# Sixteen pairs by seven products in both FFNs, the last chunk's weight sums made inside the FFN

## The chip, the cores and the metric

The kernel runs on one core of one Trainium2 chip. The metric is the device time of one execution in microseconds (us), lower is better. Before the change it is 1126.34 us, the median of 3 runs (1126.19 to 1126.67).

The engines are TensorE (PE, matmuls; its weight loads are shown as PEld), VectorE (DVE), ScalarE (ACT), GpSimd (POOL) and SyncE (SP, which only issues transfers). Each has its own queue of instructions and works through it in order; they wait for each other by semaphores.

## What is computed

A causal decoder of two layers on 512 tokens of width 1024, all in float32. Layer 0 has latent and differential attention, layer 1 dilated and stick-breaking attention; after each comes a gated FFN with a causal convolution of width 3. The change touches only the FFNs:

```python
def causal_dwconv(h, w, b):          # width 3, each channel by itself
    y = lax.conv_general_dilated(h, w[:, None, :].astype(h.dtype), (1,), [(CONV_WIDTH - 1, 0)],
                                 dimension_numbers=('NWC', 'WIO', 'NWC'), feature_group_count=c)
    return y + b

def conv_ffn(h, w_up, conv_w, conv_b, w_down):
    u = causal_dwconv(h @ w_up, conv_w, conv_b)
    gate, up = jnp.split(u, 2, axis=-1)
    return (jax.nn.silu(gate) * up) @ w_down
```

`h` is 512 x 1024, `w_up` 1024 x 5632 (2816 gates and 2816 ups), `w_down` 2816 x 1024.

## The kernel before, in words

**Float32 from parts.** Each operand is split into a high part (a cast to fp32r on ACT) and a low part (the difference, on DVE); a product is three matmuls, high by high, high by low and low by high (`mm3`, lines 315 to 317). A *unit* of weights is 128 x 1024 numbers. The class `Weights` loads it into one of three raw buffers (`wraw`, issued by SP, lines 57 and 59), then splits it (line 81 on ACT, line 82 on DVE) into one of five pairs of buffers, `wh` and `wl`. `W.depth` says how many units are prepared ahead in the order of the code.

**The FFN.** The 22 gate channels' blocks of 128 and the 22 of the ups are worked through as 22 *pairs* n = 0 to 21, a gate block and an up block each. Two pairs together form one k = n // 2 of the down product.

- Pairs 0 and 1 use the first four units.
- A *plain* pair multiplies each of its two blocks (z = 0, 1) with the whole of `x`: 8 blocks of the depth, 3 matmuls of 512 columns each; two units.
- A *seven-product* pair (function `seven`) takes gate and up as one 2 x 2 block product by the scheme of seven products in place of eight (Strassen's, in Winograd's form). Each product has 4 blocks of the depth and 3 matmuls of 256 columns. The sums of `x` blocks are made once in the FFN (`x_sums`, tiles `sums`). Sums and differences of weight blocks are not made on the engines but in memory, by accumulating transfers on POOL's queue (`sum_steps`, line 161): four arrays of sums from four arrays of blocks, `ws`, held in *chunks* of three pairs. Each chunk takes 8 transfers; step by step they depend on each other. A pair reads 7 blocks of 256 KB (line 57), so 3.5 units.

`SEVEN` says which pairs are by seven products: 4 to 17 in FFN 0 and 4 to 15 in FFN 1. The sums for FFN 0 are made while layer 0's attention runs (three calls, chunks 0 to 4), those for FFN 1 while layer 1's attention runs (line 1498). A one-element transfer from a value that is computed at the right moment (the `mark`) goes ahead and holds the first transfer back until then.

After each pair come its scaling (line 492, ACT), convolution (496 and 498, DVE), silu (502, ACT) and the products of gate and up; after every second pair the steps `second` to `fifth` form the blocks of the down product's left side. `fifth` splits one result into a tile of `g_tile` (11 of them; four hold `sums` until the last seven-product pair) and appends it to `early`. In the seven-product stage the order of PE, DVE and ACT is written by hand (`manual_schedule`); steps that find no tile free are put in `late` and run behind the stage. In the other stages a planner sets the order, from its own costs.

**The down product.** It runs over k = 0 to 10 in two parts. In the first, each step k uses `early[k]` and two units made by `down_weights` (line 351 and 354, sums of weight blocks on DVE; then the split), 24 matmuls of 512 columns into banks `acc`. For k below 3 there is one more copy and add (702 and 703). In the second part the results `later` are used; `split_later` (line 223 and 224, `gh` and `gl` from `hold`) prepares them.

**What the code's lines show.** Line 559 is a copy on ACT that stands once in every seven-product pair, line 577 another; 585 and 596 are DVE's additions of products.

## Time and profile before

| | |
|---|---|
| median of 3 runs | 1126.34 us |
| the profiled execution's own time | 1127.14 us |
| its span (first to last instruction) | 1125.4 us |
| PE busy | 1114.6 us, 99% |
| PEld busy | 955.6 us, 85% |
| DVE busy | 889.2 us, 79% |
| ACT busy | 631.0 us, 56% |
| POOL busy | 109.4 us, 10% |

In FFN 0 the seven-product pairs start at 282.88 us of the span and the down product at 467.71; in FFN 1 at 826.95 and 1013.39.

How to read the rows: a row of the timeline has start, duration, engine, line, operation, what it writes and reads with shapes, and in brackets the idle time of the engine before it and what ended it. A row of the table by stretches has for each engine the busy time and, in brackets, how many instructions; then the granted clock of PE (1.00 is full), the share of the DMA engines' time and the rate. A row of the transfers has what is written and read, the issuing queue, how many, their size and the median time from issue to landing. Matmuls overlap in PE, so their durations are longer than the distance between their starts. Line numbers are those of the kernel before.

### The profile page before, as it was taken

The page shows a single profiled execution, that of the slowest core. Times are in us where ns is not written, and L with a number is a line of the kernel's source. Part 1 is how long each engine was busy: PE and PEld are TensorE (multiplying, and loading weights), DVE is VectorE, ACT ScalarE, POOL GpSimd, SP SyncE. Part 2 cuts the span into 40 slices and gives each one's busy share as a digit, 9 for nine tenths or more (in the row PEclk, how much of TensorE's full clock was granted, in tenths as well). Part 3 has the DMA queues.
Part 4 walks back from the last instruction along what each step waited for, and adds up shares of the span by engine and source line. Part 5 has one row for each costly group of instructions (what it writes and reads, how often), then busy time and mean ns, then how long its engine had stood idle before and what let it go on. Part 6 is the DMA issues. An engine that isn't in the chain of part 4 may idle for free.

```text
span 1125.4 us, 17611 instructions
## 1 busy us (share of the span) xinstructions
PE 1114.6 (99%) x6576; PEld 955.6 (85%) x6576; DVE 889.2 (79%) x1504; ACT 631.0 (56%) x1070; POOL 109.4 (10%) x214
## 2 busy tenths in 40 slices
PE   9999999999999999999999999999999999999997
PEld 8866777898999998888888877888999999888886
DVE  6677466489899999899974476677889999789896
ACT  5565466446566665456544454565466666445662
POOL 2311133220000000000031112002000000000002
PEclk9999999999999999999999999999999999999999
DMA  8797898542556554355738999922336555334461
GB/s 296 236 256 186 246 269 204 158 135 94 161 177 187 178 185 141 108 153 164 243 98 267 300 287 291 250 77 98 94 104 196 176 182 190 111 100 144 139 206 75
DMA packets 66406, 201.48 MB, mean 179 GB/s; under 512 B 9105, under 2 KB 10257, under 8 KB 59665
## 3 DMA queue, kind: packets, MB, share of 16 engines
q1 hardware_dynamic: 56928, 143.34, 39.0%
q0 software_dynamic: 7904, 54.53, 19.0%
q10 hardware_dynamic: 1488, 2.49, 0.7%
q8 instruction: 52, 0.85, 0.3%
q14 instruction: 34, 0.27, 0.1%
HBM read 192.95 MB, written 60.85 MB: 226 GB/s over the span
## 4 chain that ended last, share of the span: by engine, by line
PE 88%; DVE 5%; DMA 2%; issue 2%; ACT 2%; POOL 0%; SPq 0%; POOLq 0%; DVEq 0%; ACTq 0%
PE u L315 12%; PE u L316 12%; PE u L317 12%; PE acc L315 4%; PE acc L316 4%; PE acc L317 4%; PE apt L315 3%; PE apt L316 3%; PE apt L317 3%; PE ao L315 2%; PE ao L317 2%; PE ao L316 2%; DVE wl L82 2%; PE sps L1115 2%; PE av L317 1%
## 5 line engine op out<-in xcount | busy, mean ns | idle before, releaser
L81 ACT CAST wh<-wraw 128x1024 fp32r<-128x1024 f32 x237 | 245.3, 1048 | 155.6 <-PE u L316 51.1
L82 DVE TENSOR_TENSOR wl<-wraw,wh 128x1024 fp32r<-128x1024 f32 x237 | 287.3, 1219 | 56.9 <-ACT wh L81 55.5
L315 PE MATMUL u<-xh,wh 128*128 128x256 f32 (+1 forms) x664 | 212.1, 319 | 0.0
L316 PE MATMUL u<-xl,wh 128*128 128x256 f32 (+1 forms) x664 | 211.8, 319 | 0.0
L317 PE MATMUL u<-xh,wl 128*128 128x256 f32 (+1 forms) x664 | 211.7, 319 | 0.0
L315 PEld LDWEIGHTS u<-xh,wh 128*128 128x128 f32 x664 | 126.5, 191 | 9.0 <-ACT wh L81 0.3
L317 PEld LDWEIGHTS u<-xh,wl 128*128 128x128 f32 x664 | 126.5, 190 | 8.9 <-DVE wl L82 0.3
L316 PEld LDWEIGHTS u<-xl,wh 128*128 128x128 f32 x664 | 126.5, 191 | 8.6
L316 PE MATMUL acc<-wl,gh 128*128 128x512 f32 (+1 forms) x250 | 96.9, 387 | 0.0
L317 PE MATMUL acc<-wh,gl 128*128 128x512 f32 (+1 forms) x250 | 96.8, 387 | 0.0
L315 PE MATMUL acc<-wh,gh 128*128 128x512 f32 (+1 forms) x250 | 96.8, 388 | 0.0
L315 PE MATMUL u<-gh,wh 128*128 128x256 f32 x312 | 88.3, 283 | 0.0
L317 PE MATMUL u<-gh,wl 128*128 128x256 f32 x312 | 88.3, 283 | 0.0
L316 PE MATMUL u<-gl,wh 128*128 128x256 f32 x312 | 88.3, 283 | 0.0
L230 POOL TENSOR_TENSOR rv<-ms,epst 128x1 f32<-128x1 f32 x39 | 12.1, 309 | 758.6 <-ACT junk L282 372.1
L492 ACT ACTIVATE y<-u,cw 128x512 f32<-128x512 f32 x88 | 67.5, 776 | 14.7 <-PE u L317 14.7
L496 DVE SCALAR_TENSOR_TENSOR y<-u,cw,y 128x511 f32<-128x511 f32 x88 | 65.0, 742 | 5.2 <-ACT y L492 5.2
L498 DVE SCALAR_TENSOR_TENSOR y<-u,cw,y 128x510 f32<-128x510 f32 x88 | 65.5, 746 | 2.3
L315 PEld LDWEIGHTS u<-gh,wh 128*128 128x128 f32 x312 | 59.9, 192 | 0.2
L316 PEld LDWEIGHTS u<-gl,wh 128*128 128x128 f32 x312 | 59.9, 192 | 0.1
L317 PEld LDWEIGHTS u<-gh,wl 128*128 128x128 f32 x312 | 59.9, 192 | 0.0
L315 PEld LDWEIGHTS acc<-wh,gh 128*128 128x128 f32 x250 | 46.9, 188 | 10.1 <-issue 0.6
(364 smaller groups left out, 2432.7 us busy)
## 6 DMA issues: line engine op xcount, KB each, us to landing
ws<-in_ffn_up_q POOLq DMA_DIRECT2D x48, 768.0 KB, 12.8
wraw<-ws SPq DMA_DIRECT2D x104, 256.0 KB, 3.0
wraw<-in_ffn_w_down SPq DMA_DIRECT2D x44, 512.0 KB, 3.6
wraw<-in_ffn_up_q SPq DMA_DIRECT2D x78, 256.0 KB, 2.9
wraw<-in_ffn_w_up SPq DMA_DIRECT2D x36, 512.0 KB, 3.7
ws<-ws POOLq DMA_DIRECT2D x16, 768.0 KB, 13.6
wraw<-in_od_w_dqk SPq DMA_DIRECT2D x12, 512.0 KB, 11.4
wraw<-in_ffn_w_down SPq DMA_DIRECT2D x22, 256.0 KB, 2.9
```

Of the source, the lines that this page charges most:

```text
L81: self.nc.scalar.copy(h[:, :w], raw[:, :w])
L82: self.nc.vector.tensor_tensor(l[:, :w], raw[:, :w], h[:, :w].bitcast(F32), ALU.subtract)
L230: POOL.tensor_tensor(v[:, :n], ms, epst[:, :n], ALU.add)
L315: PE.matmul(o, lh, rh, start=first, stop=False, skip_group_check=more)
L316: PE.matmul(o, lh, rl, start=False, stop=False, skip_group_check=more)
L317: PE.matmul(o, ll, rh, start=False, stop=last, skip_group_check=more)
L492: ACT.activation(y[:, z], u[z], AF.Identity, bias=c[:, 3:4], scale=c[:, 2:3])
L496: DVE.scalar_tensor_tensor(y[:, z, 1:], u[z][:, :S - 1], c[:, 1:2], y[:, z, 1:], ALU.mult, ALU.add)
L498: DVE.scalar_tensor_tensor(y[:, z, 2:], u[z][:, :S - 2], c[:, 0:1], y[:, z, 2:], ALU.mult, ALU.add)
L1115: PE.matmul(s_ps[:, :w], mq[h][:, i * P:(i + 1) * P], mk[h][:, :w], start=True, stop=True)
```

## The change

`SEVEN` becomes pairs 4 to 19 in both FFNs, so two plain pairs are left behind them in each. The sizes of the chunks are listed: FFN 0 has (3, 3, 3, 3, 2, 2), FFN 1 (3, 3, 3, 3, 4). The last chunk of each, `OWN`, is made inside the FFN itself, from the moment at which the gate of pair 0 has been scaled; the other chunks are made where they were. `fifth` of k = 7 takes a pair of weight buffers in place of a `g_tile`, one more step runs at once where it was put in `late`, and the lookahead behind the seven-product pairs is one less.

```diff
-SEVEN = range(4, 18), range(4, 16)
-CHUNK = 3
+SEVEN = range(4, 20), range(4, 20)
 PAIRS = [len(n) for n in SEVEN]
-CHUNKS = [-(-n // CHUNK) for n in PAIRS]
+CHUNKS = (3, 3, 3, 3, 2, 2), (3, 3, 3, 3, 4)
+PLACE = [[(c, i) for c, n in enumerate(sizes) for i in range(n)] for sizes in CHUNKS]
+OWN = (5,), (4,)
...
                 else:
-                    src = A[f"ffn_up_q{layer}"][src, c * CHUNK * P:c * CHUNK * P + n]
-                nc.gpsimd.dma_start(tiles[j][c][:n].rearrange(wide, q=4), src.rearrange(wide, q=4), accum_op=op,
+                    at = sum(CHUNKS[layer][:c]) * P
+                    src = A[f"ffn_up_q{layer}"][src, at:at + CHUNKS[layer][c] * P]
+                nc.gpsimd.dma_start(tiles[j][c][:].rearrange(wide, q=4), src.rearrange(wide, q=4), accum_op=op,
                                     max_dma_last_dim=8192)
...
-                return sums_of[layer][j - 4][i // CHUNK][i % CHUNK * P:(i % CHUNK + 1) * P]
+                c, i = PLACE[layer][i]
+                return sums_of[layer][j - 4][c][i * P:(i + 1) * P]
...
                     def fifth():
-                        g = g_tile()
+                        g = W.pair() if len(early) == HF - 4 else g_tile()
...
-                    if heavy and n < 2 * (HF - 4) + 2:
+                    if heavy and n < 2 * (HF - 3) + 2:
                         rest[3]()
                     elif heavy:
                         late.append(rest[3])
...
                             written.__exit__(None, None, None)
-                            W.depth = depth
+                            W.depth = depth - 1
...
                         if z == 0 or n != pairs[0] - 1:
                             scale(z)
+                        if n == z == 0 and OWN[layer]:
+                            ACT.copy(lead[0:1, 2 + layer:3 + layer], y[0:1, 0, 0:1])
+                            make_sums(layer, OWN[layer], lead[0:1, 2 + layer:3 + layer])
...
-                make_sums(1, range(CHUNKS[1]), lead[0:1, 1:2])
+                make_sums(1, range(4), lead[0:1, 1:2])
```

More of the change, by code (lines that the diff above doesn't have):

```diff
@@ L148, in sum_steps @@
             if layer not in sums_of:
-                sums_of[layer] = [[dpool.tile([CHUNK * P, S], F32, tag=f"ws{layer}{j}{c}", name="ws")
-                                   for c in range(CHUNKS[layer])] for j in range(4)]
+                sums_of[layer] = [[dpool.tile([n * P, S], F32, tag=f"ws{layer}{j}{c}", name="ws")
+                                   for c, n in enumerate(CHUNKS[layer])] for j in range(4)]
             tiles = sums_of[layer]
             def move(c, j, src, op):
-                n = min(CHUNK, PAIRS[layer] - c * CHUNK) * P
                 if src is None:
-                    src = tiles[0][c][:n]
+                    src = tiles[0][c][:]
                 elif src < 0:
-                    src = tiles[1][c][:n]
+                    src = tiles[1][c][:]
                 else:
-                    src = A[f"ffn_up_q{layer}"][src, c * CHUNK * P:c * CHUNK * P + n]
-                nc.gpsimd.dma_start(tiles[j][c][:n].rearrange(wide, q=4), src.rearrange(wide, q=4), accum_op=op,
+                    at = sum(CHUNKS[layer][:c]) * P
+                    src = A[f"ffn_up_q{layer}"][src, at:at + CHUNKS[layer][c] * P]
+                nc.gpsimd.dma_start(tiles[j][c][:].rearrange(wide, q=4), src.rearrange(wide, q=4), accum_op=op,
                                     max_dma_last_dim=8192)
```

## The prediction, made before the result was known

> **What bounds the kernel now.** I read the page's busy times first, then the busy time of each engine by stretches of one FFN, then the timelines of ScalarE (ACT), VectorE (DVE) and TensorE (PE) around the stage that changes, and last the table of transfers.
>
> ```profile
> PE 1114.6 (99%) x6576; PEld 955.6 (85%) x6576; DVE 889.2 (79%) x1504; ACT 631.0 (56%) x1070; POOL 109.4 (10%) x214
> ```
>
> ```profile
> core 0: us, PE busy (x) PEld busy (x) DVE busy (x) ACT busy (x) POOL busy (x), PEclk, DMA share, GB/s
> ...
> 321.00:341.00 20.00, 20.00 (x169) 20.00 (x168) 18.77 (x27) 13.18 (x18) 0.00 (x0) 1.00 0.60 184
> ...
> 436.00:447.00 11.00, 11.00 (x50) 9.13 (x49) 8.96 (x12) 5.53 (x8) 0.00 (x0) 1.00 0.23 73
> ...
> 475.00:486.00 11.00, 11.00 (x51) 9.09 (x50) 11.00 (x14) 6.64 (x8) 0.00 (x0) 1.00 0.48 139
> 486.00:497.00 11.00, 11.00 (x50) 9.13 (x49) 11.00 (x15) 6.46 (x8) 0.00 (x0) 1.00 0.58 183
> 497.00:508.00 11.00, 11.00 (x51) 9.09 (x50) 8.69 (x12) 5.30 (x7) 0.00 (x0) 1.00 0.51 142
> 508.00:519.00 11.00, 11.00 (x50) 9.13 (x49) 10.27 (x15) 7.31 (x11) 0.00 (x0) 1.00 0.30 93
> 519.00:530.00 11.00, 11.00 (x50) 8.98 (x49) 9.93 (x14) 7.14 (x10) 0.00 (x0) 1.00 0.73 243
> ```
>
> The stretches are FFN 0: 321 to 341 lies in the pairs by seven products, 436 to 447 in the plain pairs, 475 to 530 in the first part of the down product. PE is busy without a break at a granted clock of 1.00 in all of them, so PE's own work is the path. DVE is the one engine near it: 94% in the seven-product pairs, all of the time from 475 to 497.
>
> How long a pair takes is read from ACT, which does one thing at a fixed place of each pair.
>
> ```profile
> 310.43 0.36 ACT L559 COPY u<-u 128x256 f32<-128x256 f32 x1 [2.01 <-PE u L317]
> ...
> 411.21 0.36 ACT L559 COPY u<-u 128x256 f32<-128x256 f32 x1 [1.90 <-PE u L317]
> ...
> 440.49 1.05 ACT L81 CAST wh<-wraw 128x1024 fp32r<-128x1024 f32 x1 [2.39 <-PE u L316]
> ...
> 462.25 1.05 ACT L81 CAST wh<-wraw 128x1024 fp32r<-128x1024 f32 x1 [3.19 <-PE u L316]
> ```
>
> L559 runs once per seven-product pair; from 310.43 to 411.21 are ten pairs, so one takes 10.08 us. The two casts each wait for PE to free a weight buffer, four plain weight units apart: 21.76 / 4 = 5.44 us a unit, 10.88 a plain pair.
>
> **The change part by part.** *Six pairs change form (two in FFN 0, four in FFN 1).* A plain pair is 2 halves x 8 blocks x 3 = 48 matmuls of 512 columns, one each 227 ns; the other form is 7 x 4 x 3 = 84 of 256, one each 120 ns. A pair saves 10.88 - 10.08 = 0.80 us of PE, six save 4.8 us, all of it on the path as long as PE stays fed. The Trainium skill (TensorE: Matmul & The Clock Gate, Back-to-back issue gap) gives N/2.4 + 2.5 ns for an isolated gap: by that 10.36 and 9.17 us a pair, 7.1 us for six. The rows of this case are 13 ns a matmul above it in both forms, and I take the rows.
>
> *DVE and ACT in those pairs.* A seven-product pair has 3.5 weight units to split where a plain one has 2. DVE stays at 94% there, so a longer stretch of the same kind costs nothing. PE stands in front of it: if that cover went, each of the 1.5 extra splits would cost 1.2 us.
>
> *What comes after the seven-product pairs.* Now FFN 0 has four plain pairs there and FFN 1 six; afterwards both have two. They are where DVE gets ahead of PE. Also, one of the five weight buffers is taken from pair 16 on by a split result (the eighth of `early`, until step 7 of the down product), so four are left, and the lookahead is cut from 5 to 4. The down product's tightest place today:
>
> ```profile
> 467.71 0.39 PE L315 MATMUL acc<-wh,gh 128*128 128x512 f32 x1
> ...
> 467.70 1.05 ACT L81 CAST wh<-wraw 128x1024 fp32r<-128x1024 f32 x1 [0.97 <-PE u L316]
> ...
> 468.78 1.23 DVE L82 TENSOR_TENSOR wl<-wraw,wh 128x1024 fp32r<-128x1024 f32 x1 [0.85 <-ACT wh L81]
> 469.92 0.74 DVE L496 SCALAR_TENSOR_TENSOR y<-u,cw,y 128x511 f32<-128x511 f32 x1
> ...
> 473.62 0.42 DVE L525 TENSOR_TENSOR y<-y 128x256 f32<-128x256 f32 x1
> 473.96 0.41 DVE L528 TENSOR_TENSOR y<-y 128x256 f32<-128x256 f32 x1
> ...
> 479.98 1.22 DVE L82 TENSOR_TENSOR wl<-wraw,wh 128x1024 fp32r<-128x1024 f32 x1
> 481.12 0.68 DVE L351 TENSOR_TENSOR wraw<-wraw 128x512 f32<-128x512 f32 x1
> 481.72 1.22 DVE L82 TENSOR_TENSOR wl<-wraw,wh 128x1024 fp32r<-128x1024 f32 x1
> ```
>
> Call 467.71, the first matmul of the down product, s. A step k of it takes 24 matmuls, 5.44 us, and uses its second unit first (wl in its second matmul, 0.23 later). Step 3 needs it at s + 16.32 + 0.23 = 484.26; its split (481.72) ends at 482.94, 1.3 us early. In FFN 1 it is the same place:
>
> ```profile
> 1013.39 0.39 PE L315 MATMUL acc<-wh,gh 128*128 128x512 f32 x1
> ...
> 1027.39 1.22 DVE L82 TENSOR_TENSOR wl<-wraw,wh 128x1024 fp32r<-128x1024 f32 x1
> ```
>
> There 1028.61 against 1029.94, also 1.3, though six plain pairs lie ahead: the buffers, not the plain pairs, set it. With four buffers the second unit of step 1 gets the buffer that the last plain unit frees, so its cast starts at s (today that cast belongs to step 2) and DVE takes it 1.08 later. In the changed program's order of instructions DVE has between it and step 3's second split, that one included: 5 pieces of 1024 columns, 2 of the convolution, 10 of 512 and 4 of 256. From start to start these take 1.14, 0.70, 0.60 and 0.34 (481.12 less 479.98, 0.04 under the duration 0.74, 481.72 less 481.12, 473.96 less 473.62): 5.70 + 1.40 + 6.00 + 1.36 = 14.5. The step 1 split starts at s + 1.08 and holds DVE for 1.14, the 14.5 follow, the last split among them with its full 1.22: its end is at s + 1.08 + 1.14 + 14.5 + 0.08 = s + 16.8, 0.2 late; today's stretch from 468.78 to 482.94 runs 0.3 over the same kind of sum, so 0.5 late. Bounds: nothing (DVE loses none of its 1.3 us) to 2.3 (below). I take 0.5 for each FFN, 1.0. Behind it come, for steps 4 to 8, 10 pieces of 1024, 2 of 768 (under 1.14 each), 17 of 512 and 3 of 256: 11.4 + 2.3 + 10.2 + 1.0 = 24.9 us against PE's 5 x 5.44 = 27.2, so DVE recovers. FFN 1 also gets one split (1.14) put behind its last seven-product pair, as FFN 0 has it today; it lies under the plain pairs.
>
> *The last chunk's sums, made in the plain pairs.* Eight transfers in memory for each FFN, 512 KB in FFN 0 and 1 MB in FFN 1, a one-element transfer ahead of them, and one ACT copy of one element (under L559's 0.36 us, beside PE). POOL has nothing else to do until the end of the FFN (POOL is at 0.00 in every stretch above), so nothing queues behind their waits there. The other chunks keep their sizes and places.
>
> ```profile
> 260.21 2.78 ACT L492 ACTIVATE y<-u,cw 128x512 f32<-128x512 f32 x4 [0.87 <-PE u L317]
> 282.88 0.28 PE L315 MATMUL u<-xh,wh 128*128 128x256 f32 x1
> ...
> 804.29 2.79 ACT L492 ACTIVATE y<-u,cw 128x512 f32<-128x512 f32 x4 [0.88 <-PE u L317]
> 826.95 0.28 PE L315 MATMUL u<-xh,wh 128*128 128x256 f32 x1
> ```
>
> ```profile
> q0 software_dynamic: 7904, 54.53, 19.0%
> ...
> ws<-in_ffn_up_q POOLq DMA_DIRECT2D x48, 768.0 KB, 12.8
> wraw<-ws SPq DMA_DIRECT2D x104, 256.0 KB, 3.0
> wraw<-in_ffn_w_down SPq DMA_DIRECT2D x44, 512.0 KB, 3.6
> ...
> wraw<-in_od_w_dqk SPq DMA_DIRECT2D x12, 512.0 KB, 11.4
> ...
> ws<-ws POOLq DMA_DIRECT2D x2, 512.0 KB, 4.8
> ```
>
> They start when the first pair is scaled (261 and 805) and form a chain of six dependent steps, 4.8 to 12.8 us each by these rows: done by 265 + 77 = 342 in FFN 0 and 886 in FFN 1 at the latest, needed at 282.88 + 14 x 10.08 = 424 and 826.95 + 12 x 10.08 = 948. In time. But they run on into the seven-product pairs, whose loads (60% of the DMA time) they share. 19.0% of 1125 us for 54.5 MB is 3.9 us of all engines per MB: 33 us in FFN 1, 16 in FFN 0, of which the lightly loaded plain pairs can take half or more. PE is 3.9 us behind the splits (first plain unit: split ends 420.13, used at 424.0) and that absorbs a short delay:
>
> ```profile
> 418.90 1.23 DVE L82 TENSOR_TENSOR wl<-wraw,wh 128x1024 fp32r<-128x1024 f32 x1 [1.32 <-ACT wh L81]
> ```
>
> Bounds 0 to 6.3 us (below); I take 0.4, near the lower end, because only one or two transfers are in flight where the 11.4 us row had a crowd.
>
> *Moved loads.* On SP, each changed pair issues seven loads of 256 KB in place of two of 512 KB; loads on SP wait for raw buffers as now. Cost nothing, under PE.
>
> Sum: 4.8 - 1.0 - 0.4 = 3.4 us. The profiled execution took 1127.14 with a span of 1125.4, 0.8 above the median; span 1122.0, median 1126.34 - 3.4 = **1122.9**. What a measurement can tell is about 0.2%, 2.25 us.
>
> **The rivals.** *All of it arrives:* DVE reaches step 3 in time, the transfers are hidden. For it: 1.3 us in hand at step 3 today. Against: four buffers. 1126.34 - 4.8 = 1121.5.
>
> *DVE becomes the bound of the down product.* DVE is full from 475 to 497, and idle 11 + 11 + 11 - 8.69 - 10.27 - 9.93 = 4.1 us from 497 to 530, waiting for loads and casts. If these waits stay, with four buffers, steps 4 to 8 need 24.9 + 4.1 = 29.0 against 27.2: 1.8 more, 2.3 for each FFN. 4.8 - 4.6 - 0.4 = -0.2: 1126.5, no change.
>
> *Slower: the transfers starve the seven-product pairs.* Three raw buffers turn over once per load, cast and split; 8.64 us are there for three units (3 x 2.88), cast and split take 2.3, so it decides when loads take over 6.3 us on average. They take 3.0 now (3.6 for 512 KB), and 11.4 for 512 KB in the stretch where the other sums are made. At 11.4 each round of three loses 11.4 + 2.3 - 8.64 = 5.1 us; two rounds in FFN 1, less the 3.9 of the lead, give 6.3: 1122.5 + 6.3 = 1128.8. The Trainium skill (DMA: Bandwidth & Descriptors, Queues, rings and completion order) says that each DMA engine goes round between the queues that have work, a packet at a time; by that a load does not wait for a whole transfer, but shares with it, which the rise from 3.6 to 11.4 agrees with. Against it: at most two of the new transfers at a time.
>
> *The sums come late,* so pairs 16 to 19 wait and the time grows by what is missing: they have 62 us in hand at least by the bounds above. Some 1128 and up.
>
> **How the numbers follow.** All of it 0.20; forecast 0.42 (1121.9 to 1124.2 by itself); DVE bound 0.18; starved loads 0.13; late or something not seen 0.07. Faster by 0.2% (under 1124.1): the first and nearly all of the second, 0.60. Within: the rest of the second and most of the third, 0.20. Slower: 0.20. The range 1121.3 to 1128 leaves out the dearer part of the last two.
>
> **What would show it.** In the profile after: L315 to L317 together 216 more; L559's copy (some lines lower) every 10.08 us, 32 times; first `acc` matmul of FFN 0 near 465.9; no DVE wait on `in_ffn_w_down` beyond 1 us; a PE gap of about 0.5 us some 16 us behind each first `acc`. Wrong: PE gaps in the first seven-product pairs of FFN 1 with ACT waiting on `wraw` loads above 6 us (starved), gaps at every step of the down product (DVE bound), or another time per pair than 10.08.

## The result, and the profile after

| | median us | lowest to highest | runs |
|---|---|---|---|
| before | 1126.12 | 1125.62 to 1126.67 | 6 |
| after | 1130.86 | 1128.11 to 1132.55 | 6 |

After against before is 1.0043, 95% interval 1.0032 to 1.0053: slower by 4.7 us, where 1122.9 was forecast. The profiled execution after took 1130.34 us, with a span of 1128.2. The two profiled executions, which the stages below are read from, differ by 2.8 us of span: that of before lies 0.8 above its median, that of after 0.5 below its own.

First the page of the kernel after, busy times, software queue and a load's landing (issues, KB each, median us). PE has 6792 - 6576 = 216 matmuls more, as the step on the pairs had it. The software queue moved 67.12 MB where it moved 54.53.

```profile
PE 1112.5 (99%) x6792; PEld 963.3 (85%) x6792; DVE 901.7 (80%) x1525; ACT 643.6 (57%) x1093; POOL 119.1 (11%) x232
...
q0 software_dynamic: 9760, 67.12, 23.6%
...
wraw<-ws SPq DMA_DIRECT2D x128, 256.0 KB, 3.0
```

The timeline of PE after, at the edges of the stages: the first seven-product matmul of FFN 0, its first and its last `acc`, and the same of FFN 1 (the lines stand two lower than before, so L317 to L319 are the old L315 to L317).

```profile
281.94 0.28 PE L317 MATMUL u<-xh,wh 128*128 128x256 f32 x1
...
465.17 0.39 PE L317 MATMUL acc<-wh,gh 128*128 128x512 f32 x1
...
572.20 0.39 PE L319 MATMUL acc<-gh,gl 128*128 128x512 f32 x1
...
825.48 0.28 PE L317 MATMUL u<-xh,wh 128*128 128x256 f32 x1
...
1014.83 0.39 PE L317 MATMUL acc<-wh,gh 128*128 128x512 f32 x1
...
1120.77 0.28 PE L319 MATMUL acc<-wh,gl 128*128 128x256 f32 x1
```

Of before the same places are in the prediction, but for the last `acc` of each FFN:

```profile
573.67 0.39 PE L317 MATMUL acc<-gh,gl 128*128 128x512 f32 x1
...
1118.19 0.28 PE L316 MATMUL acc<-wl,gh 128*128 128x256 f32 x1
```

The last one read off for the last `acc` of FFN 1 is 1118.31, one matmul (0.12) behind this row. So the time went:

| stage | before | after | difference |
|---|---|---|---|
| FFN 0, first seven-product matmul to first `acc` | 184.83 | 183.23 | -1.60 |
| FFN 0, first to last `acc` | 105.96 | 107.03 | +1.07 |
| FFN 0's last `acc` to FFN 1's first seven-product matmul | 253.28 | 253.28 | 0 |
| FFN 1, first seven-product matmul to first `acc` | 186.44 | 189.35 | +2.91, where -3.20 was due |
| FFN 1, first to last `acc` | 104.92 | 105.94 | +1.02 |

The rest is -0.94 ahead of FFN 0's stage, where the code is the same but for the small copy and the start of FFN 0's own transfers, and +0.37 behind the last `acc`.

Where FFN 1's stage loses 6.1 us is seen in the copy that ACT makes once in each seven-product pair (L561, formerly L559). The timeline of ACT after:

```profile
832.92 0.37 ACT L561 COPY u<-u 128x256 f32<-128x256 f32 x1
845.11 0.37 ACT L561 COPY u<-u 128x256 f32<-128x256 f32 x1
857.55 0.36 ACT L561 COPY u<-u 128x256 f32<-128x256 f32 x1 [1.90 <-PE u L319]
868.01 0.36 ACT L561 COPY u<-u 128x256 f32<-128x256 f32 x1
879.28 0.36 ACT L561 COPY u<-u 128x256 f32<-128x256 f32 x1 [2.48 <-PE u L319]
889.36 0.36 ACT L561 COPY u<-u 128x256 f32<-128x256 f32 x1 [1.16 <-PE u L319]
```

The steps are 12.19, 12.44, 10.46, 11.27 and 10.08. Against 10.08 that is 2.11 + 2.36 + 0.38 + 1.19 = 6.04 us, and after 879 nothing more. Stretches of the kernel after over the first two of these pairs (columns: us; PE, PEld, DVE, ACT, POOL busy; granted clock; DMA share; GB/s):

```profile
825.50:836.00 10.50, 10.50 (x89) 10.50 (x88) 6.67 (x13) 4.56 (x8) 0.82 (x1) 1.00 0.91 298
836.00:842.60 6.60, 6.60 (x57) 6.60 (x56) 4.88 (x6) 4.00 (x6) 0.00 (x0) 1.00 1.03 236
842.60:846.00 3.40, 0.41 (x4) 0.23 (x2) 1.81 (x3) 2.82 (x4) 0.54 (x1) 0.91 1.09 355
846.00:849.00 3.00, 3.00 (x15) 3.00 (x16) 2.44 (x4) 0.58 (x1) 0.00 (x0) 0.53 0.88 319
```

And of before at the same place:

```profile
826.90:835.00 8.10, 8.10 (x69) 8.06 (x69) 4.76 (x7) 3.50 (x7) 0.00 (x0) 1.00 0.21 75
835.00:842.60 7.60, 7.60 (x66) 7.60 (x65) 6.97 (x12) 6.29 (x9) 0.00 (x0) 1.00 0.48 140
```

The DMA engines are full where they were at a quarter to a half. PE stops for 3 us; the 3 us behind that touch 15 matmuls, where 27 would fit (one each 0.12 us, and two over the edges), at a granted clock of 0.53. Who keeps PE waiting is told by the chain of work between 825 and 870 after (start, us, what):

```profile
815.90 16.04 DMA wraw<-in_ffn_up_q
831.97 1.06 ACT wh L82
833.05 1.23 DVE wl L83
...
834.67 8.36 DMA wraw<-ws
843.11 1.05 ACT wh L82
844.19 1.23 DVE wl L83
845.42 0.35 DVE u L587
...
851.39 9.19 DMA wraw<-in_ffn_up_q
```

Three loads of 256 KB on the path took 16.04, 8.36 and 9.19 us; the page's median is 3.0. What PE itself waits for is not the split but L587 (formerly L585), the addition of products that stands behind the split in DVE's order and whose bank PE goes on with (timeline of PE after):

```profile
845.90 0.56 PE L317 MATMUL u<-gh,wh 128*128 128x256 f32 x1 [2.99 <-DVE u L587]
```

Beside the loads the transfers for the last chunk's sums run, issued by POOL (timeline of POOL after, each with the wait for the one before it):

```profile
834.22 0.82 POOL L162 DMA_DIRECT2D ws<-in_ffn_up_q  x1 [9.04 <-DMA ws<-ws]
...
851.27 0.82 POOL L162 DMA_DIRECT2D ws<-in_ffn_up_q  x1 [7.46 <-DMA ws<-ws]
```

The chain's first transfer starts at 807.74 and its last at 851.27; the other long gap, 1.32 us at 867, has the load of 9.19 us in its chain, issued beside the last transfer.

### The profile page after: what moved, and what is told of

Same layout as the page of the kernel before. It is cut to its first block, busy times and chain, and to the rows that moved or that the text cites. A ratio compares the mean times of both kernels' runs of the same rounds, so it can differ in the third digit from the quotient of the medians.

```text
span 1128.2 us, 18178 instructions
## 1 busy us (share of the span) xinstructions
PE 1112.5 (99%) x6792; PEld 963.3 (85%) x6792; DVE 901.7 (80%) x1525; ACT 643.6 (57%) x1093; POOL 119.1 (11%) x232
## 3 DMA queue, kind: packets, MB, share of 16 engines
q0 software_dynamic: 9760, 67.12, 23.6%
## 4 chain that ended last, share of the span: by engine, by line
PE 80%; DVE 9%; DMA 5%; issue 3%; ACT 2%; POOL 0%; SPq 0%; POOLq 0%; DVEq 0%; ACTq 0%
PE u L317 11%; PE u L319 11%; PE u L318 11%; DVE wl L83 4%; PE apt L317 3%; PE apt L318 3%; PE acc L317 3%; PE apt L319 3%; PE acc L318 2%; PE acc L319 2%; DMA wraw<-in_ffn_up_q 2%; PE ao L317 2%; PE ao L319 2%; PE ao L318 2%; DMA wraw<-in_ffn_w_down 2%
## 5 line engine op out<-in xcount | busy, mean ns | idle before, releaser
L83 DVE TENSOR_TENSOR wl<-wraw,wh 128x1024 fp32r<-128x1024 f32 x246 | 298.6, 1220 | 44.9 <-ACT wh L82 43.4
L82 ACT CAST wh<-wraw 128x1024 fp32r<-128x1024 f32 x246 | 254.8, 1047 | 128.1 <-PE u L318 24.2
L317 PE MATMUL u<-xh,wh 128*128 128x256 f32 (+1 forms) x640 | 195.3, 305 | 0.0
L319 PE MATMUL u<-xh,wl 128*128 128x256 f32 (+1 forms) x640 | 195.3, 305 | 0.0
L318 PE MATMUL u<-xl,wh 128*128 128x256 f32 (+1 forms) x640 | 195.1, 305 | 0.0
L319 PEld LDWEIGHTS u<-xh,wl 128*128 128x128 f32 x640 | 122.5, 191 | 5.5 <-DVE wl L83 0.7
L317 PEld LDWEIGHTS u<-xh,wh 128*128 128x128 f32 x640 | 122.6, 192 | 4.9
L317 PE MATMUL u<-gh,wh 128*128 128x256 f32 x384 | 109.6, 285 | 4.3 <-DVE u L587 4.3
L318 PE MATMUL u<-gl,wh 128*128 128x256 f32 x384 | 109.4, 285 | 0.0
L319 PE MATMUL u<-gh,wl 128*128 128x256 f32 x384 | 109.3, 285 | 0.0
L317 PE MATMUL acc<-wh,gh 128*128 128x512 f32 (+1 forms) x234 | 90.6, 389 | 0.5 <-DVE uu L704 0.5
L319 PE MATMUL acc<-wh,gl 128*128 128x512 f32 (+1 forms) x234 | 90.8, 388 | 0.0
L317 PEld LDWEIGHTS u<-gh,wh 128*128 128x128 f32 x384 | 74.3, 193 | 4.8 <-ACT u L561 4.7
L318 PEld LDWEIGHTS u<-gl,wh 128*128 128x128 f32 x384 | 74.3, 194 | 0.1
L319 PEld LDWEIGHTS u<-gh,wl 128*128 128x128 f32 x384 | 74.3, 194 | 0.0
L162 POOL DMA_DIRECT2D ws<-in_ffn_up_q x66 | 47.8, 726 | 155.6 <-DMA ws<-ws 75.1
```

What stands on the lines that cost most here:

```text
L82: self.nc.scalar.copy(h[:, :w], raw[:, :w])
L83: self.nc.vector.tensor_tensor(l[:, :w], raw[:, :w], h[:, :w].bitcast(F32), ALU.subtract)
L162: nc.gpsimd.dma_start(tiles[j][c][:].rearrange(wide, q=4), src.rearrange(wide, q=4), accum_op=op, max_dma_last_dim=8192)
L317: PE.matmul(o, lh, rh, start=first, stop=False, skip_group_check=more)
L318: PE.matmul(o, lh, rl, start=False, stop=False, skip_group_check=more)
L319: PE.matmul(o, ll, rh, start=False, stop=last, skip_group_check=more)
```

## The experiments

Each kernel here was run beside the kernel before. This table holds the stages as they are read above, from the profiled execution of each, and the times; the sections below take them one by one. "Due" is before less 0.80 us for each changed pair.

| run | FFN 0 sevens | FFN 0 `acc` | FFN 1 sevens | FFN 1 `acc` | median us | ratio to before (95%) |
|---|---|---|---|---|---|---|
| before | 184.84 | 105.96 | 186.44 | 104.92 | | |
| due with 16 and 16 pairs | 183.24 | | 183.24 | | | |
| after | 183.23 | 107.03 | 189.35 | 105.94 | 1130.86 | 1.0043 (1.0032 to 1.0053) |
| sums in the attention | 183.22 | 106.70 | 183.26 | 106.53 | 1149.71 | 1.0208 (1.0194 to 1.0222) |
| no transfers | 183.25 | 106.96 | 183.24 | 105.79 | 1123.78 | 0.9981 (0.9972 to 0.9991) |
| FFN 0 only | 183.36 | 106.71 | 186.46 | 104.92 | 1125.51 | 0.9998 (0.9989 to 1.0007) |
| two small chunks | 183.24 | 106.86 | 193.04 | 106.30 | 1129.83 | 1.0033 (1.0023 to 1.0044) |
| buffers only | 184.91 | 106.03 | 186.46 | 105.75 | 1127.81 | 1.0016 (1.0008 to 1.0025) |
| moved to idle | 183.22 | 106.24 | 183.24 | 106.21 | 1130.68 | 1.0038 (1.0026 to 1.0050) |
| fourteen pairs | 183.24 | 107.50 | 184.98 | 105.06 | 1126.43 | 1.0005 (0.9996 to 1.0013) |
| FFN 0 with 1 MB | 190.97 | 106.81 | 187.71 | 106.44 | 1135.86 | 1.0089 (1.0067 to 1.0110) |
| between the norms | 183.65 | 106.89 | 183.22 | 106.48 | 1125.22 | 0.9994 (0.9985 to 1.0003) |
| spaced | 183.32 | 106.95 | 189.88 | 106.30 | 1132.18 | 1.0054 (1.0041 to 1.0066) |
| one split later | 183.38 | 105.91 | 183.22 | 105.26 | 1122.83 | 0.9974 (0.9965 to 0.9983) |
| two splits later | 183.26 | 106.16 | 183.22 | 105.86 | 1124.18 | 0.9983 (0.9974 to 0.9992) |

### No transfers: are they the cause?

```diff
-OWN = (5,), (4,)
+OWN = (5,), ()
...
-                c, i = PLACE[layer][i]
+                c, i = PLACE[layer][i - 12 if layer and i > 11 else i]
```

> The changed kernel without the last chunk's transfers in FFN 1: pairs 16 to 19 of FFN 1 load the sums of pairs 4 to 7, so the same loads are issued and the eight transfers are left out (the sums of four pairs are those of others). Theory 'starved loads': FFN 1's seven-product stage takes 183 to 184 us, attention is as before, time 1126.1 - 4.8 + 2 = 1123.3. Rival 'four buffers': stage 188 us or more, time near 1130. The difference to the kernel with the transfers in attention is what they cost there.

This kernel leaves out the sums of pairs 16 to 19, so it does not compute the function; it stands here for its time alone.

1123.78. FFN 1's stage takes 183.24 us, to the hundredth what was due. Against after, 1130.86 - 1123.78 = 7.1 us by the medians (6.9 when each is taken against the before of its own set of runs): that is the price of eight transfers of 1 MB. In the profiled executions 6.1 of it is in the stage. The stretch that was full in the kernel after, in this kernel:

```profile
825.50:836.00 10.50, 10.50 (x89) 10.46 (x88) 7.12 (x13) 4.88 (x8) 0.00 (x0) 1.00 0.30 90
836.00:842.60 6.60, 6.60 (x58) 6.60 (x57) 6.00 (x8) 5.57 (x8) 0.00 (x0) 1.00 0.48 160
```

The DMA share is at 0.30 and 0.48 instead of 0.91 and 1.03, with the same weight loads. The four weight buffers are those of the kernel after, so they are not what FFN 1's stage lost by.

How little a late load needs to stop PE is seen in the same pair of this kernel, on DVE and on PE:

```profile
842.19 0.42 DVE L587 TENSOR_TENSOR u<-u,y 128x256 f32<-128x256 f32 x1
```

```profile
842.93 0.28 PE L317 MATMUL u<-gh,wh 128*128 128x256 f32 x1
```

The addition ends at 842.61, 0.3 us before PE goes on with its bank. It comes right behind a split (L83). By these rows a load that lets this split start more than 0.3 us late stops PE, however far the splits themselves are ahead of PE.

### FFN 0 only

```diff
-SEVEN = range(4, 20), range(4, 20)
+SEVEN = range(4, 20), range(4, 16)
...
-CHUNKS = (3, 3, 3, 3, 2, 2), (3, 3, 3, 3, 4)
+CHUNKS = (3, 3, 3, 3, 2, 2), (3, 3, 3, 3)
...
-OWN = (5,), (4,)
+OWN = (5,), ()
...
-                        g = W.pair() if len(early) == HF - 4 else g_tile()
+                        g = W.pair() if layer == 0 and len(early) == HF - 4 else g_tile()
...
-                            W.depth = depth - 1
+                            W.depth = depth - (layer == 0)
```

> Only FFN 0 has 16 pairs by seven products, with its own chunk of two pairs (512 KB a transfer) made inside; FFN 1 as before with 12. Both theories: FFN 0's seven-product stage starves nothing (no gap over 0.1 us in the changed kernel's trace), gains 1.6, and its down product loses 1.1 (PE gaps of 0.6 and 0.4 us where the banks are freed): 1126.1 - 0.5 = 1125.6, with a small spread. If it comes out above 1126.5, or spreads like the changed kernel (4.4 us over six runs), then FFN 0's transfers starve too, in executions other than the profiled one.

1125.51, as expected and within what can be told from no change. FFN 0's stage gains what was due, with eight transfers of 512 KB running at its start, and its `acc` part gives back 0.75.

### Sums in the attention

```diff
-OWN = (5,), (4,)
+OWN = (5,), ()
...
-                make_sums(1, range(4), lead[0:1, 1:2])
+                make_sums(1, range(5), lead[0:1, 1:2])
```

> The changed kernel, but FFN 1's last chunk of sums (four pairs, 1 MB a transfer) is made with the other four while layer 1's attention runs; FFN 0 as in the changed kernel. Theory 'starved loads': the 6.1 us that FFN 1's seven-product stage lost in the profiled run (189.4 us from its first matmul to the down product, where 186.4 - 3.2 = 183.2 were due) come from the eight transfers beside its loads. Then the stage takes 183 to 184 us here, its PE gaps of 3.2 and 1.5 us are gone, and the time is 1126.1 - 4.8 + 2 (both down products) + 0 to 2 (attention, where eight more transfers now run) = 1123.3 to 1125.3, with a spread over the runs as small as before. Rival 'four buffers': the stage lost because only four weight buffers are left from pair 16 on and the longer stage runs DVE dry; then it still takes 188 us or more and the time stays near 1130.

1149.71, 24 us over the upper end of what was expected. FFN 1's stage takes 183.26, as due, but PE stands still for 23.3 us in the attention, which the expectation had at 0 to 2. There the heads' statistics, 16 KB, are sent through memory (function `exchange`). The transfers between 736.5 and 761 in this kernel, one of them by its issue (KB, us to landing):

```profile
on<-stat SPq DMA_DIRECT2D x1, 16.0 KB, 22.6
```

and between 728.5 and 735 in the kernel after, where no sums run at that time:

```profile
on<-stat SPq DMA_DIRECT2D x1, 16.0 KB, 1.8
```

What waits for it in this kernel (waits from 725 to 765):

```profile
DVE sm L1646 <- DMA on<-stat: 23.4, 1, 23.4
```

### Two small chunks

```diff
-CHUNKS = (3, 3, 3, 3, 2, 2), (3, 3, 3, 3, 4)
+CHUNKS = (3, 3, 3, 3, 2, 2), (3, 3, 3, 3, 2, 2)
...
-OWN = (5,), (4,)
+OWN = (5,), (4, 5)
```

> The changed kernel with FFN 1's last chunk of four pairs cut into two chunks of two: sixteen transfers of 512 KB in place of eight of 1 MB, issued in turn, inside FFN 1 as before. The bytes are the same, each transfer is half. If what starves the loads is the work of the DMA engines (bytes), the stage still loses some 6 us: time 1129 to 1132. If it is the length of one transfer that a load finds ahead of it, half: 1126 to 1128.

1129.83, as the theory of bytes has it, and in the profiled execution FFN 1's stage lost 193.04 - 183.24 = 9.8 us (that execution was the longest of the ten, 1133.63; the shortest took 1126.29). The same bytes in sixteen transfers of half the size cost about as much: the length of one transfer is not what hurts.

### One megabyte in FFN 0, and half a megabyte in FFN 1

```diff
-CHUNKS = (3, 3, 3, 3, 2, 2), (3, 3, 3, 3, 4)
+CHUNKS = (3, 3, 3, 3, 4), (3, 3, 3, 3, 4)
...
-OWN = (5,), (4,)
+OWN = (4,), (4,)
...
-                moves = sum_steps(0, range(3, 5))
+                moves = sum_steps(0, range(3, 4))
```

> The changed kernel with FFN0's last chunk of four blocks instead of two, so that its own eight transfers carry 1 MB each as in FFN1; the chunk made ahead of FFN0 is one smaller in number, the total of bytes is the same. If the size of the transfers beside the seven-product pairs decides, FFN0's seven-product stage lengthens from 183.2 us to about 187 to 190, and the time is 1135 to 1138. If the loss of FFN1 has a cause of its own there (its x stores, its place behind the attention), FFN0 stays at 183.2 to 184 and the time at 1131.

1135.86 (1131.79 to 1141.13). FFN 0's stage, untouched so far, takes 190.97 in the profiled execution (the longest of the six), 7.7 over what is due; it shows the same picture, in stretches:

```profile
296.70:306.70 10.00, 7.62 (x64) 7.44 (x62) 6.69 (x9) 6.72 (x10) 0.54 (x1) 0.99 1.03 278
306.70:316.70 10.00, 10.00 (x72) 10.00 (x73) 8.55 (x11) 5.01 (x7) 0.81 (x1) 0.84 0.94 256
```

Besides, FFN 0 begins 4.8 us later in that execution (first `u` matmul at 239.79 against 234.98). Of the chunks made in the attention the last is gone in this kernel; why FFN 0 begins later stays open, and the median's 5.0 us over after can't be divided between the two. FFN 1, whose code is that of after, loses 187.71 - 183.24 = 4.5 us in this execution.

The opposite, FFN 1 with 14 pairs and half the transfer size:

```diff
-SEVEN = range(4, 20), range(4, 20)
+SEVEN = range(4, 20), range(4, 18)
...
-CHUNKS = (3, 3, 3, 3, 2, 2), (3, 3, 3, 3, 4)
+CHUNKS = (3, 3, 3, 3, 2, 2), (3, 3, 3, 3, 2)
```

> The changed kernel with 14 instead of 16 pairs by seven products in FFN1, so that its own chunk has two blocks: eight transfers of 512 KB at the same place instead of 1 MB. If the bytes decide, the chain is over near 840 us, about as in FFN0, and FFN1's stage takes 184.84 us with a gap of under 1 us: 1126.0 less 0.5 (FFN0 alone) less 1.6 (two pairs at 0.80) plus 1.0 (down part) makes 1124.9, with up to 1 us more. If the number and place of the transfers decide, FFN1 loses some 6 us as before: 1131.

1126.43, 0.5 above the upper end of the theory of bytes; in the profiled execution FFN 1's stage takes 184.98 where 184.84 was due. The eleven runs go from 1124.71 to 1129.32, so some may lose more there than the profiled one. In the profiled executions the loss in a seven-product stage is 0.0 and 0.1 us for eight transfers of 512 KB, 6.1, 7.7 and 4.5 for eight of 1 MB, 9.8 for sixteen of 512 KB. So it goes by the bytes and not by the length of a transfer.

Which bytes is told by POOL's timelines. With 512 KB only the last three transfers fall beside the seven-product pairs: in the kernel with fourteen pairs they are issued at 824.30, 833.39 and 837.22, and the stage starts at 826.27. That is 1.5 MB. With 1 MB in the kernel after it is the last four, issued from 824.63 to 851.27, with the stage from 825.48: 4 MB. The rest of each chain runs beside the plain pairs, all but the end of one transfer in the kernel after. A smaller chain is also over earlier, and these runs do not separate the two.

### Moved to idle

The mark and four transfers go behind the second exchange in the attention, four behind the last norm ahead of FFN 1.

```diff
-OWN = (5,), (4,)
+OWN = (5,), ()
...
                             share(st12, by_r, 1, slice(0, 4))
+                            own = sum_steps(1, (4,), shares[1][0:1, 0, 0:1])
+                            for move in own[:5]:
+                                move()
...
                     r = mean_square(X[i][:])
+                    for move in own[5:]:
+                        move()
```

> The changed kernel with the same eight transfers of 1 MB for FFN1's last chunk at another time: the mark and four of them behind the second statistics exchange in layer 1's attention (about 745 us), the other four behind the last rstd (about 787 us), where the DMA engines are at 0.2 to 0.4. Theory that the transfers starve the weight loads because they run beside seven-product pairs: FFN1's seven-product stage takes 183.2 us as without the transfers, and the time is 1123.8 (1123.0 to 1124.6), below both kernels. Rival, the sums of this chunk cost the same wherever they are put: a stall appears at the end of the attention or at the first plain pairs, and the time stays at 1126 to 1131.

1130.68. The stage is at 183.24, as expected, but the part between the FFNs is 7.1 us longer (260.4 against 253.3, from FFN 0's last `acc` to FFN 1's first seven-product matmul): four loads of the output product's weights started at 745.6, a microsecond behind the transfers. Their landing from 740 to 765 in this kernel, with the wait:

```profile
wraw<-in_ffn_w_up SPq DMA_DIRECT2D x4, 512.0 KB, 10.9
```

```profile
ACT wh L82 <- DMA wraw<-in_ffn_w_up: 5.6, 1, 5.6
```

In the kernel after the same four take

```profile
wraw<-in_ffn_w_up SPq DMA_DIRECT2D x4, 512.0 KB, 3.8
```

An average of the DMA share over 10 us (0.16, 0.48 there) did not show that loads with little time in hand lay inside it. The rival of that run, a stall at the end of the attention, was right.

### Between the norms

The transfers start two by two behind the rows of the attention's output product, behind those loads.

```diff
-OWN = (5,), (4,)
+OWN = (5,), ()
...
                         r = rstd(ms[:, 0:1], ms[:, 1:2])
+                        if n == 0:
+                            own = sum_steps(1, (4,))
+                        for move in own[:(2, 0, 2, 1)[n]]:
+                            own.pop(0)()
...
                     r = mean_square(X[i][:])
+                    for move in own:
+                        move()
```

> The changed kernel with FFN1's own eight transfers of 1 MB started between the rows of the output product ahead of FFN1: two behind the first row's rstd (about 762 us), two behind the third's (about 773), one behind the fourth's (about 781), three behind the last rstd (from 787 on), so that the last is issued near 803. By the windows of the changed kernel the DMA engines are at 0.14, 0.25, 0.52 and 0.10 in the four stretches of 10 us from 760 to 800, and the next loads that PE needs at once come behind 804. If transfers cost only where weight loads that are due run beside them, the seven-product stage takes 183.2 us, the part from 760 to 825 stays within 1 us, and the time is 1123.8 to 1124.8. Rival, the two weight loads and the x stores of that stretch are late, or rstd waits behind a transfer on POOL: 2 to 6 us lost ahead of FFN1, 1126 to 1130.

1125.22, 5.6 us under after, 0.4 above the expected range, and not to be told from before. FFN 1's stage is at 183.22, and the plain pairs ahead of it are 0.5 longer (47.57 against 47.06). The DMA engines are full there too, and PE is hardly touched (a stretch of this kernel):

```profile
780.00:790.00 10.00, 9.56 (x80) 9.18 (x80) 7.50 (x10) 3.81 (x8) 3.53 (x6) 1.00 1.04 276
```

The same bytes cost 7.1 us in one place and about 1.4 (1125.22 - 1123.78) in the other; nearly half of that is the 0.7 by which this execution's `acc` part of FFN 1 is longer than that without transfers.

### Spaced

```diff
-                            make_sums(layer, OWN[layer], lead[0:1, 2 + layer:3 + layer])
+                            own = sum_steps(layer, OWN[layer], lead[0:1, 2 + layer:3 + layer])
+                            with tc.manual_schedule(engines={POOL.engine}):
+                                for _ in range(5 if layer else len(own)):
+                                    own.pop(0)()
...
                         left = seven(n, left)
+                        if own and n % 2 == 0:
+                            ACT.copy(lead[0:1, 8 + n:9 + n], lead[0:1, 0:1])
+                            with tc.manual_schedule(engines={POOL.engine}):
+                                POOL.tensor_copy(lead[0:1, 40 + n:41 + n], lead[0:1, 8 + n:9 + n])
+                                own.pop(0)()
```

> The changed kernel with the last four of FFN1's eight transfers held back: each waits for a small ACT copy at the end of the seven-product pairs 4, 6, 8 and 10, so that one starts every 20 us (near 836, 856, 876 and 896) instead of every 9 us; the first four stay at FFN1's start. If it is the backlog of the DMA engines (1.0 busy from 825 to 845) that starves the loads, there is room between transfers (0.6 for the loads, about 0.4 for one transfer in 20 us), the gaps of 3.2 and 1.5 us shrink to under 1 us in all and the time is 1123.8 to 1125. If any single 1 MB transfer beside a due load stalls PE, four gaps of 1 to 3 us remain and the time is 1127 to 1131.

1132.18. The theory of a backlog falls: with one transfer every 20 us FFN 1's stage takes 189.88, 6.6 over what is due, as much as back to back. A stretch of this kernel with no full DMA engines and still PE gaps:

```profile
865.00:875.00 10.00, 8.44 (x69) 8.06 (x67) 7.01 (x9) 6.24 (x11) 0.00 (x0) 1.00 0.64 221
```

The other theory, that a single transfer of 1 MB beside a due load stalls PE, is about right. The first spaced transfer (837.27) costs nothing. The next three are issued at 858.03, 881.44 and 902.35, and the chain of work of this kernel (850 to 935) has a load of 256 KB that starts 3.0 us behind each of them:

```profile
861.03 7.94 DMA wraw<-ws
...
884.44 5.39 DMA wraw<-ws
...
905.35 6.76 DMA wraw<-ws
```

From 862 to 930 PE has gaps that cost up to 1.5 us each and wait for DVE's addition L587 or, once, for the other one, L598: what stops PE is again the addition behind a split that came late. In after, in this kernel and with two small chunks all gaps of over 1 us in FFN 1's stage end so. With 1 MB in FFN 0 the two long gaps of FFN 0's stage do too, but the one of FFN 1's, 2.57 us, ends with the cast of a weight (ACT L82). That DVE, at 94%, needs several pairs to make good such a delay would explain why the gaps go on between the transfers; it is argued and not shown.

### Buffers only

The kernel before with the buffer part of the change alone: `fifth`, the limit on `n` in `seven`, and the lookahead.

```diff
-                        g = g_tile()
+                        g = W.pair() if len(early) == HF - 4 else g_tile()
...
-                    if heavy and n < 2 * (HF - 4) + 2:
+                    if heavy and n < 2 * (HF - 3) + 2:
...
-                            W.depth = depth
+                            W.depth = depth - 1
```

> The kernel before with only the buffer part of the change: the fifth sum of the seventh early unit takes a pair of the weights' own buffers, and the weights keep one buffer less from there to the end of the FFN (4 instead of 5); pairs and sums as before. Theory A, the buffers cause the loss of about 1 us in each down product: both down parts lengthen as in the changed kernel (FFN0 from 106.0 to about 107.0 us, FFN1 from 104.9 to about 105.9), the time is about 1128. Theory B, the loss comes from having seven-product pairs up to two or four pairs nearer to the down product, so that DVE arrives later: the down parts stay within 0.2 us of before and the time is about 1126.1.

1127.81, as theory A has it, but the `acc` parts agree with A in FFN 1 alone (+0.83), in FFN 0 they are unmoved (+0.07). In FFN 1 the wait that was predicted for step 3 is there, 16.5 us behind the first `acc` of this kernel: the second matmul below starts 0.56 us behind the first, where 0.23 is the rule, so 0.34 is lost (its timeline of PE):

```profile
1029.60 0.39 PE L315 MATMUL acc<-wh,gh 128*128 128x512 f32 x1
1030.16 0.50 PE L316 MATMUL acc<-wl,gh 128*128 128x512 f32 x1 [0.18 <-DVE wl L82]
```

The matmul behind it loses 0.11 more, and 0.32 are lost at the bank evictions near 1076.5.

The other part of the 1.9 us by the medians isn't found in its stages; the profiled execution of before lies 0.8 above its own median, which accounts for some of it.

### One split later, two splits later

The kernel between the norms, with one of the splits of `later` tiles taken from ahead of the first bank evictions (L704) to behind them, in both FFNs:

```diff
                     if k < 3:
...
-                    if k >= HF - 3:
+                    if k >= HF - 2:
                         split_later()
```

> The kernel with the transfers between the norms, and in both down products one of the eleven splits of later g tiles (some 1.6 us of DVE and 1.4 us of ACT) moved from ahead of the first bank evictions to behind them: two instead of three splits in the last three steps of the first part, one more at its end. If the loss of about 1 us in each down product is DVE being 1 us behind PE where the uu banks are added up, the gaps there (0.5 and 0.4 us in FFN0, 0.7 and 0.4 in FFN1) go, the down parts come back to 106.0 and 105.0 us, and the time is 1123.3 (1122.9 to 1124.0), faster than before. If the loss comes from loads that are issued later by one buffer, the gaps stay and the time is 1125.2; if the moved split makes the second part late, 1126 to 1127.

1122.83, 3.1 us under before in the same set of runs (1125.98), faster than both kernels and 2.4 under the kernel between the norms, as the first theory has it. The first of the additions at the bank evictions on DVE, after and then with one split later; the first `acc` stands at 465.17 and 465.14:

```profile
524.10 0.68 DVE L704 TENSOR_TENSOR uu<-uu,acc 128x512 f32<-128x512 f32 x1
```

```profile
523.03 0.68 DVE L704 TENSOR_TENSOR uu<-uu,acc 128x512 f32<-128x512 f32 x1
```

Counted from the first `acc`, DVE is 1.0 us earlier, and what PE of the kernel after waited for there

```profile
526.57 0.50 PE L317 MATMUL acc<-wh,gh 128*128 128x512 f32 x1 [0.46 <-DVE uu L704]
...
527.77 0.51 PE L317 MATMUL acc<-gh 128*128 128x512 f32 x1 [0.23 <-DVE uu L704]
```

is gone: no wait for L704 of over 0.1 us is left in either FFN (105.91 and 105.26). With `k >= HF - 1`, two splits behind:

> As the one before, with two of the eleven splits moved behind the first bank evictions. If one was enough, this adds nothing at the evictions, and the three splits left at the end of the first part may hold up the second by up to 1.6 us: 1123.3 to 1125. If DVE is still behind with one moved, this one is the faster by what is left of the gaps. If the loss is in the loads, both stay at 1125.2.

1124.18, within what was expected, and slower than one: waits for L704 come back, which cost up to 0.3 us each (106.16 and 105.86).

The `acc` parts scatter by execution, each being read from one. FFN 0's, with the same code in ten of these kernels (after to spaced, but for buffers only), goes from 106.24 to 107.50; FFN 1's, in the eight of them with 16 pairs there, from 105.79 to 106.53. One split later is below both ranges.

## Why the prediction was wrong

*Pairs: right.* 0.80 us a pair; the stages without disturbance came out at 183.22 to 183.26 in FFN 1 (183.24 due) and FFN 0 at 183.23. The spacing of 227 and 120 ns that the rows gave holds. The formula that the prediction took from the Trainium skill (TensorE: Matmul & The Clock Gate, Back-to-back issue gap) would have made it 7.1 us for six pairs, an estimate; without the transfers the two stages gained 4.8. The rows lie 11 ns a matmul above that formula (227 against 216, 120 against 109), not 13 as the prediction has it; nothing hangs on it.

*DVE in those pairs: right only as long as nothing disturbs.* PE does stand in front of it, but DVE also has additions to make in time for PE, and one of them in every second pair has 0.3 us in hand.

*Transfers: the step that failed.* "I take 0.4, near the lower end, because only one or two transfers are in flight" measured 7.1 us, over the upper bound of 6.3. One transfer in flight was enough: the fourth of the chain landed at 830.67 (issued at 817.31), from then on each ran alone, and the loads of 8.36 and 9.19 us were issued after that. From 825.5 to 849 the DMA engines were filled, and 256 KB loads took 6.3 and 5.5 us (median, `ws` and `in_ffn_up_q`) where they take 3.1 and 2.8 without transfers. The rows of 11.4 us for a load were the nearest and should have been taken; the number in flight was no reason to go to the other end. The cover that was to absorb a delay, "PE is 3.9 us behind the splits", was not there either, in two ways. It was misread: PE does the first four matmuls of that plain unit from 419.65 on, ahead of the rest, and loads the `wl` of the split that ends at 420.13 at once, having waited for it (timeline of PEld before).

```profile
420.18 0.19 PEld L317 LDWEIGHTS u<-xh,wl 128*128 128x128 f32 x1 [0.33 <-DVE wl L82]
```

And within the seven-product pairs it is not the splits that PE meets first but the addition behind them in DVE's order, L587, which ends 0.3 us ahead of PE in every second pair when nothing disturbs. The rule quoted from the Trainium skill (DMA: Bandwidth & Descriptors, Queues, rings and completion order), engines going round between queues a packet at a time, agrees with loads that get slower by sharing. In FFN 0 the estimate was right, 0.0, for half the bytes, of which 1.5 MB fell beside the seven-product pairs.

*The condition of the starved rival*, loads of over 6.3 us on average, was reached by the one median (6.3) and not by the other (5.5), and is not what decides: in the spaced run loads of 256 KB landed in 4.2 and 4.5 us (medians, 855 to 875) and the loss was the same. Single late loads count, through the addition that waits behind their split. Its picture was right, gaps in FFN 1's first seven-product pairs with ACT waiting for `wraw`. Its 1128.8 is 2.1 below the time: the transfers are 0.8 dearer than its 6.3, the down products 1.1 dearer than its 1.0. That its 6.3 came so near is luck in part: it takes loads of 11.4 us, where the medians were 6.3 and 5.5, and deducts the 3.9 of a lead that did not cover.

*Down product: too small, and mostly the wrong place.* 0.5 us for each FFN at step 3 measured 1.07 and 1.02. In the kernel after at most 0.1 us is lost at step 3; the wait is at the end of the first part, where DVE comes late to add up the banks: PE waits for L704, and with DVE 1.0 us earlier the wait is gone. "DVE recovers" was worked out for steps 4 to 8 and stopped there, short of the evictions. Step 3's wait was seen once, with the buffers alone. What makes DVE late stays open. The buffers alone lengthen FFN 1's part by 0.83 and FFN 0's by 0.07, but over half of the 0.83 is lost at step 3, where the kernel after loses nearly nothing. FFN 1 with fourteen pairs has the buffers too, and two plain pairs fewer, and is only 0.14 longer than before (105.06). Keeping all five buffers beside the new arrangement was not tried.

*Sums in time, SP's loads, POOL:* right; no pair waited for its sums.

With the transfers moved and one split put later the change takes 1122.83 us, beside the 1122.9 of the forecast. That is luck and no confirmation of its sum, whose two deductions were both wrong for the kernel as it stood.

## What to carry to other kernels

Price a background transfer by what it does to loads that are due while it runs, not by how many transfers are in flight: the same 8 MB cost 7.1 us beside weight loads that were due, about 1.4 us when they ran some 40 us earlier, and 26 us (1149.71 - 1123.78) beside a 16 KB exchange on which everything waited. How much a late load may be late is not told by how far the weights are prepared ahead, but by the next thing that its consumer has to do in time: here a split that waited for its load held up an addition with 0.3 us in hand. Spreading the transfers out did not help in this stage (6.6 us against 6.1); moving them out of it did. And follow a buffer that is taken away to the end of its stage, to the next place where the busy engine has to be in time.

## What was not expected of the hardware

After a PE gap of 2.99 us the granted clock was 0.53 over the stretch of 3 us shown above. Its matmuls start 0.21 us apart in place of 0.12, and the gap cost another 1.4 us. The Trainium skill (TensorE: Matmul & The Clock Gate, Part 1: The HAM clock gate) gives an idle window of about 3.4 us for the clock to fall; here it fell after a gap a little shorter than that. The length of the gap alone does not decide: with 1 MB in FFN 0 the clock also fell after gaps of 2.38 and 1.98 us (0.50 from 330.40 to 333.50, behind the second), and with two small chunks not after one of 2.54. Gaps of 1.32 us and of 0.46 us in the kernel after left it at 1.00.

A transfer of 16 KB took 22.6 us in place of 1.8 while the software queue was busy. It goes in small packets: in those 24.5 us of the run with the sums in the attention (queue: packets, MB, share)

```profile
q1 hardware_dynamic: 1056, 0.03, 4.1%
```

1056 packets carry 0.03 MB, some 30 bytes each on average. By the rule of the Trainium skill (DMA: Bandwidth & Descriptors, Queues, rings and completion order), a packet at a time from each queue, small packets could each wait for a large one of the other queue. That would fit, but it is argued and not shown: larger or fewer packets were not tried.

The time of a kernel with starved loads scatters: over 4.4 us for after, 7.3 with two small chunks, 9.3 with 1 MB in FFN 0, where the five sets of runs of before span 1.1 to 2.7 us and those without the transfers 2.4.
